# Moving one matmul operand, and all that lies behind it in on-chip memory, to rounder start addresses

## The chip, the cores and the metric

The kernel runs on one core of one Trainium2 chip. Its on-chip memory (SBUF) has 128 partitions, and a tile is a stretch of bytes that begins at the same address in each of them. TensorE (PE) multiplies, VectorE (DVE), ScalarE (ACT) and GpSimd (POOL) work element by element, SyncE (SP) issues the weight transfers. The metric is the device time of one execution in microseconds (us), as the median of three runs.

## The reference, cut to what is computed

Two transformer blocks over 512 tokens of 1024 channels, in float32. The first block runs two layers of feed-forward, a mixer of three attention branches, feed-forward; the second is one layer of a dilated attention mixer with a convolution, and a feed-forward. The feed-forward is the bulk of the work:

```
def swiglu_ffn(x, g, w_gu, w_down):
    h = rms_norm(x, g)
    gate, up = jnp.split(h @ w_gu, 2, axis=-1)
    return (jax.nn.silu(gate) * up) @ w_down
...
for l in range(DEPTH):                                   # first block, DEPTH = 2
    x = x + 0.5 * swiglu_ffn(x, ffn1_norm[l], ffn1_w_gu[l], ffn1_w_down[l])
    x = x + hybrid_mixer(rms_norm(x, mix_norm[l]), ...)  # q, k, v, gates: all products of h
    x = x + 0.5 * swiglu_ffn(x, ffn2_norm[l], ffn2_w_gu[l], ffn2_w_down[l])
...
x = x + rms_norm_2(merged @ w_mix_out, g_post_mix)       # second block, one layer
x = x + rms_norm_2(swiglu_ffn_2(h, w_ffn_in, w_ffn_out), g_post_ffn)
```

## The kernel before

**Tiles.** Three tiles share each partition. `ar` holds matmul operands of type float32r (the ring of prepared weights at R_W, the feed-forward's inner values at R_O, keys and queries). `af` holds float32: weight staging at A_ST, constants at A_C, parameters, small statistics at A_SM, then x at A_X (4096 elements) and scratch behind it at A_Y. In the attention stages the same place behind A_X holds other scratch (M_IQ to M_DQ, and for the second block a list of names U, A, S, P, B, V, PT, T). `h` is the transposed, normalized activation that most products read: eight chunks of 128 channels by 512 tokens, first the high parts, then the low parts. The build puts `ar` at byte 16512 of a partition, `af` at 125056 (both multiples of 128), and `h` at 196384, which is 32 above a multiple of 128. x begins at 147744, 32 above a multiple of 64; of the second block's scratch U does too, and what stands behind U begins 16 above a multiple of 64.

**Products.** `mm3` (L168 to L174) makes one product of a 128x128 weight tile with a chunk of 512 tokens in float32's precision by three matmuls: weight high with activation high (L172), weight high with activation low (L173), weight low with activation high (L174). The weight tile is loaded as the stationary operand, the activation streams as the moving one. In the feed-forward (`gen_ffn`, L244) `up` streams `h`, and `down` streams the inner values from `ar`. Each of five feed-forwards has 22 chunks x 2 x 8 x 3 = 1056 matmuls that stream `h`. Each of the two mixers (`gen_mix`, L386) has 30 units of 24 (`tunit`, L437), the second block's mixer (`gen_mix2`, L1021) 68 units of 24, its output product (`gen_merge2`, L1366) 192. The `group` units of the mixer turn it round: there `h` is the stationary operand and the weights stream.

**Order.** Weights come in 550 units of 512 KB. SP loads a unit into staging, ACT copies it to the ring (L141), DVE makes the low part (L142); the loop is tied to how far the products have come. The order on each engine is fixed when the kernel is built. In the mixers the attention (side stream) is woven into the products (main stream). `bias_rows` (L1005), in the first feed-forward, computes three small tables `t` in scratch at A_Y + 3584 + 2328 and POOL writes each to DRAM 128 times over (`dr_b`, L1019). In `gen_mix2` DVE filters eight chunks with 31 taps each (L1132), a tap starting 4 bytes behind the one before.

Of the kernel before, what the change touches and what calls it, by code (L numbers as in the profile page):

```python
# [26 lines left out]

# [1 line left out]
R_W = 0  # L29
# [18 lines left out]
A_SM = A_RB + 512  # L48
A_X = A_SM + 328
A_Y = A_X + 4096  # L50
# [10 lines left out]
M_DQ = M_PT + 1024  # L61
A_SIZE = M_DQ + 1024

# [30 lines left out]
def const_r():  # L94
    """Stationaries: -1 where row >= column; -1 all over; identity; the strict-past mask."""
    c = np.zeros((128, 512), np.float32)
    p = np.arange(128)
    c[:, 0:128] = np.where(p[:, None] >= p[None, :], -1.0, 0.0)
    c[:, 128:256] = -1.0
    c[:, 256:384] = np.eye(128)  # L100
    c[:, 384:512] = np.where(p[:, None] < p[None, :], 0.0, NEG)
    return c
# [7 lines left out]
class Build:  # L110
# [10 lines left out]

# [1 line left out]
    def r(self, off, n):  # L123
# [4 lines left out]

# [1 line left out]
    def w_dma(self):  # L130
# [29 lines left out]

# [1 line left out]
    def bank(self, ring):  # L162
# [3 lines left out]

# [1 line left out]
    def mm3(self, out, w, a, start, stop, act_stationary=False):  # L168
# [7 lines left out]
    def split(self, hi, lo, src, scale=None):  # L176
        """hi + lo = src * scale, to float32's precision."""
        if scale is None:
            self.nc.scalar.activation(hi, src, AF.Copy)  # L179
            self.nc.vector.tensor_tensor(lo, src, hi, op=ALU.subtract)  # L180
        else:
            self.nc.scalar.activation(hi, src, AF.Copy, scale=scale)
            self.nc.vector.scalar_tensor_tensor(lo, src, scale, hi, op0=ALU.mult, op1=ALU.subtract)  # L183
# [6 lines left out]

# [1 line left out]
    def sq_acc(self, m, src, acc, tmps, apart=False):  # L192
# [19 lines left out]
    def stats_a(self, accs, ps, eps=1e-6, ts=range(4)):  # L212
        """Column sums of the accs into token-major rstd [128, 4]."""
        nc = self.nc
# [12 lines left out]
    def bcast(self, cols, dg, ps, out):  # L227
        """out[:, t*128 + i] = cols[i, t] on every partition."""
        nc = self.nc
        for t in range(cols.shape[-1]):  # L230
            nc.vector.tensor_scalar_mul(dg[:, 128 * t:128 * t + 128], self.f(A_C + C_ID, 128), cols[:, t:t + 1])
        nc.tensor.matmul(ps, lhsT=self.f(A_C + C_ONE, 128), rhs=dg, start=True, stop=True)
        nc.scalar.activation(out, ps, AF.Copy)
# [8 lines left out]

# [1 line left out]
    def gen_ffn(self, wgu, wdn, l, done, halves=None):  # L244
# [41 lines left out]
        def down(grp, cs):  # L286
# [15 lines left out]
            if grp == 0 or not halves:  # L302
                return
            # the last channels a half of the tokens at a time
            tl = {}
# [21 lines left out]
    def ffn_add(self, gain, last=None):  # L327
        """x += 0.5 * rstd * product; the second half also readies the next operand."""
        nc = self.nc
# [12 lines left out]
    def drive(self, main, side=None):  # L342
        """Program order is priority: the side stream goes first, the main one as far as it is waited for."""
        alive = True
# [17 lines left out]
    def behind(self, first, ins):  # L362
        """A product issues behind the one that opens its bank (the first, when there is none yet)."""
        if first is None:
# [6 lines left out]
    @contextlib.contextmanager  # L371
    def late(self, by):
        """Work that other work goes before where both are ready."""
        tc = self.tc
        p = tc.cur_priority
        tc.cur_priority = max(0, p + by)
        yield
        tc.cur_priority = p
# [5 lines left out]

# [1 line left out]
    def gen_mix(self, l):  # L386
# [68 lines left out]

        # compressed branch: the rows (parity, channel) of its first product's operand
        stk = self.r(R_O + 2048, 6144)
# [60 lines left out]
        for m in range(8):  # L518
            for br in range(3):
# [5 lines left out]
                n += 1  # L525
        # the first branch's part of the merge, in the operand's place
        self.mt = self.h_tile(F32)
# [13 lines left out]
    def merged(self, m):  # L541
        """Where the merge of a chunk of channels gathers."""
        return self.mt[:, 512 * m:512 * m + 512]

    def h_tile(self, dtype=F32R):
        """The products' operand; while none is there, the merge's sums."""
        return self.hp.tile([128, 8192 if dtype == F32R else 4096], dtype, name="h", tag="h")

# [1 line left out]
    def rope(self, x, co, si, h, tmp):  # L550
        """x: [128, b, n, >= 2h], co/si: [128, b, 2h]."""
        nc = self.nc
# [11 lines left out]
    def norm_heads(self, x, nh, gain, sq, sm):  # L564
        """x: [128, nh, 64] in place: rms norm over the last axis, times gain."""
        nc = self.nc
# [14 lines left out]
    def one_gain(g):  # L581
        """The same gain for every head."""
        return lambda x: [(x, g[:, None, :].to_broadcast([g.shape[0], x.shape[1], 64]))]
# [4 lines left out]
    def tpose_dup(self, ps, src, tmp, rep=2):  # L588
        """src [128 tokens, n, d]: each [tokens, d] transposed into a column block, rep times down the partitions."""
        _, n, d = src.shape  # L590
# [7 lines left out]
    def gen_idx(self, l):  # L598
# [61 lines left out]

        # the key of the sparse branch
        dk = g1[:, :, 32:96]
# [5 lines left out]
        self.split(self.r(R_KD, 512), self.r(R_KD + 512, 512), ps)  # L668
        # gates of the three branches
        ng = g1[:, :, 8:32]  # L670
# [43 lines left out]
    def sb_pair(self, hp):  # L714
        """Two heads of the stick-breaking branch, key blocks from the last to the first."""
        nc = self.nc
# [43 lines left out]
    def attn_pair(self, q, k, mask, n, gate, v, out, first):  # L760
        """Two heads over n keys: out[channel, token] += gated softmax times values, a head in each half of the rows."""
        nc = self.nc
# [42 lines left out]
    def q2_prep(self, b, src, nh):  # L805
        """Transposed [hi; lo] queries of one block of tokens: [128, nh * 128]."""
        nc = self.nc
# [27 lines left out]
    def q_prep(self, o, nh, g, sm):  # L835
        """Queries of 4 * nh heads at o: norm and rotation in place."""
        self.norm_heads(self.f(o, 256 * nh).rearrange("p (n d) -> p n d", d=64), 4 * nh,
# [4 lines left out]
    def gen_nsa(self, l):  # L842
# [8 lines left out]
        def prep(b):  # L851
            """Queries, and the compressed branch's numerators, transposed."""
            q2 = self.q2_prep(b, q4[:, b], 8)
# [102 lines left out]

# [1 line left out]
    def gen_merge(self, l, gain):  # L958
# [44 lines left out]

# [1 line left out]
    def bias_rows(self):  # L1005
        """Relative-position bias rows of every head, to DRAM."""
        nc = self.nc
# [107 lines left out]
    def conv(self, c, u):  # L1115
        """Causal depthwise filter of one chunk of channels, a tap at a time in the background."""
        nc = self.nc
# [25 lines left out]
    def gen_attn2(self):  # L1143
# [30 lines left out]
        def tok(g):  # L1174
            """The statistics in DRAM, [token, group, kind, head], as group g's layout has the tokens."""
            d = self.dr_s
# [4 lines left out]
        for hp in range(4):  # L1181
# [23 lines left out]
            if hp < 3:  # L1205
                load_bias(hp + 1)
            # statistics of the three groups meet token by token
            d = self.dr_s
# [93 lines left out]
    def gen_ln(self):  # L1302
        """Layer norm over channels of the filtered signal, silu, split for the product."""
        nc = self.nc
# [33 lines left out]
    def post(self, y, next_gain, rb, ts=range(4), pool=()):  # L1338
        """x += rms_norm(y) * gain, y transposed with the gain already in it, its squares summed."""
        nc = self.nc  # L1340
# [82 lines left out]

# [1 line left out]
    def run(self, upto=99, start=0):  # L1425
        tc, nc, ap = self.tc, self.nc, self.ap
        with tc.tile_pool(name="sb", bufs=1) as sb, tc.tile_pool(name="hp", bufs=1) as self.hp, \
# [56 lines left out]
            o = M  # L1484
            for n, sz in (("U", 1084), ("A", 1024), ("S", 512), ("P", 3840), ("B", 1024), ("V", 1536), ("PT", 1024), ("T", 2048)):
                self.m2[n] = o
# [17 lines left out]
def tile_t(v):  # L1504
    """[..., 1024] -> [128, 8] per vector, side by side."""
    v = np.asarray(v, np.float32).reshape(-1, 8, 128)
# [3 lines left out]
def par_array(inp):  # L1510
    """Small parameters, one [128, PAR] array per phase."""
    out = np.zeros((3, 128, PAR - 80), np.float32)
# [24 lines left out]
def bias_consts():  # L1537
    """Rows of one-hot buckets by position, 383 or 255 long, and what is added: 0, or NEG where no key is."""
    c = np.zeros((32, 2, 3, 384), np.float32)
# [45 lines left out]
```

## Time and profile before

| | |
|---|---|
| median of 3 runs | 3584.28 us (3582.41 to 3585.07) |
| span of the profiled execution | 3581.1 us |
| PE busy | 3481.8 us, 97% |
| DVE, ACT, POOL busy | 2001.0, 1316.6, 320.8 us |
| share of PE on the chain that ended last | 90% |
| of it, the three lines of `mm3` | 81% |

The span runs from the first to the last instruction of the program; the 3.2 us between it and the median lie around it. A matmul's own time in the trace is longer than its share of the engine, since the next one starts while it drains: the pace of PE is read from the starts of neighbours. Operands stand as out<-in, so `pb<-h,ar` is a matmul that reads `h` and `ar`.

### The profile page before, as it was taken

Reading aid. Unit: us, or ns where it says so; the run is one execution under the profiler, and the core shown is the slowest. Engines: PE = TensorE matmul, PEld = TensorE weight load, DVE = VectorE, ACT = ScalarE, POOL = GpSimd, SP = SyncE. Lnnn points to the kernel's source line nnn. Section 1 sums busy time; section 2 is a strip of 40 time slices with the busy share of each in tenths; the row PEclk is TensorE's granted clock in tenths of the full one; section 3 lists DMA queues with packets and bytes.
Section 4 is the critical chain, followed back from the end, with each engine's and each line's share of the span. In section 5 each row is a group of like instructions: output and inputs, shape, how many; then the busy total and the mean of one; then the engine's idle time right before and its main releaser. Section 6 shows DMA issues by size and latency. Waiting matters only on the chain.

```text
span 3581.1 us, 43236 instructions
## 1 busy us (share of the span) xinstructions
PE 3481.8 (97%) x16884; PEld 2802.7 (78%) x16884; DVE 2001.0 (56%) x3733; ACT 1316.6 (37%) x2234; POOL 320.8 (9%) x355
## 2 busy tenths in 40 slices
PE   7899999999999999999999999999999999999997
PEld 5688888776788888888787768888877777878886
DVE  4243488566543344434876666433488988544334
ACT  3222354356332233223544464222334443443222
POOL 2000100011300010001000104000111112210002
PEclk9899999999999999999999999999999999999999
DMA  6722332331322222223322314222332224522221
GB/s 148 116 94 94 119 94 86 103 114 62 121 90 98 94 97 89 99 94 112 95 89 101 114 38 147 94 94 94 114 100 86 81 78 142 182 77 94 95 94 54
DMA packets 100814, 357.05 MB, mean 100 GB/s; under 512 B 14168, under 2 KB 16984, under 8 KB 99808
## 3 DMA queue, kind: packets, MB, share of 16 engines
q1 hardware_dynamic: 81504, 290.49, 24.1%
q0 software_dynamic: 18144, 61.76, 6.8%
q8 instruction: 132, 2.16, 0.2%
q10 hardware_dynamic: 960, 2.04, 0.2%
q14 instruction: 74, 0.61, 0.1%
HBM read 320.05 MB, written 32.08 MB: 98 GB/s over the span
## 4 chain that ended last, share of the span: by engine, by line
PE 90%; issue 3%; DMA 3%; DVE 2%; ACT 1%; POOL 1%; another core or an unknown queue 0%; DVEq 0%; ACTq 0%; POOLq 0%
PE pb L172 27%; PE pb L173 27%; PE pb L174 27%; DMA af<-wst 2%; PE pb L801 1%; PE pb L777 1%; PE pb L793 1%; PE pb L1193 1%; PE pb L737 1%; PE pb L1290 1%; PE pb L1266 1%; PE pb L595 0%; PE pb L756 0%; DMA af<-x 0%; PE pb L751 0%
## 5 line engine op out<-in xcount | busy, mean ns | idle before, releaser
L172 PE MATMUL pb<-h,ar 128*128 128x512 f32 x2848 | 1132.8, 401 | 34.6 <-ACT ar L141 16.4
L141 ACT ACTIVATE ar<-af 128x1024 fp32r<-128x1024 f32 x550 | 582.5, 1059 | 1565.1 <-PE pb L173 993.2
L174 PE MATMUL pb<-h,ar 128*128 128x512 f32 x2848 | 1140.7, 401 | 0.1
L173 PE MATMUL pb<-h,ar 128*128 128x512 f32 x2848 | 1140.1, 400 | 0.0
L142 DVE TENSOR_TENSOR ar<-af,ar 128x1024 fp32r<-128x1024 f32 x550 | 687.2, 1250 | 448.6 <-ACT ar L141 435.6
L172 PEld LDWEIGHTS pb<-h,ar 128*128 128x128 f32 x2848 | 540.8, 190 | 167.3 <-ACT ar L141 17.3
L174 PEld LDWEIGHTS pb<-h,ar 128*128 128x128 f32 x2848 | 540.6, 190 | 130.4 <-issue 3.2
L173 PEld LDWEIGHTS pb<-h,ar 128*128 128x128 f32 x2848 | 540.7, 190 | 129.0 <-issue 3.2
L173 PE MATMUL pb<-ar 128*128 128x512 f32 (+1 forms) x1254 | 484.0, 386 | 1.2 <-DVE ar L183 1.2
L174 PE MATMUL pb<-ar 128*128 128x512 f32 (+1 forms) x1254 | 483.3, 386 | 0.0
L172 PE MATMUL pb<-ar 128*128 128x512 f32 (+1 forms) x1254 | 482.4, 387 | 0.6 <-DVE af L779 0.5
L200 POOL TENSOR_TENSOR af<-af 128x512 f32<-128x512 f32 (+1 forms) x76 | 109.6, 1442 | 1857.6 <-ACT af L198 1846.5
L172 PEld LDWEIGHTS pb<-ar 128*128 128x128 f32 x1254 | 235.7, 188 | 49.8 <-DVE af L779 1.2
L173 PEld LDWEIGHTS pb<-ar 128*128 128x128 f32 x1254 | 235.8, 188 | 48.9 <-DVE ar L183 2.4
L174 PEld LDWEIGHTS pb<-ar 128*128 128x128 f32 x1254 | 235.7, 188 | 46.8
L263 DVE TENSOR_TENSOR af<-pb,af 128x512 f32<-128x512 f32 x110 | 75.7, 691 | 317.2 <-PE pb L174 316.1
L261 DVE TENSOR_TENSOR af<-pb,af 128x512 f32<-128x512 f32 x110 | 75.5, 691 | 264.4 <-PE pb L174 249.3
L1132 DVE SCALAR_TENSOR_TENSOR af<-af 128x512 f32<-128x512 f32 x240 | 179.5, 748 | 3.6
L172 PE MATMUL pb<-ar,h 128*128 128x256 f32 (+1 forms) x448 | 134.1, 299 | 0.0
L173 PE MATMUL pb<-ar,h 128*128 128x256 f32 (+1 forms) x448 | 133.2, 297 | 0.0
L174 PE MATMUL pb<-ar,h 128*128 128x256 f32 (+1 forms) x448 | 132.4, 296 | 0.0
L180 DVE TENSOR_TENSOR ar<-af,ar 128x512 fp32r<-128x512 f32 (+4 forms) x178 | 114.4, 649 | 16.3 <-ACT ar L179 15.6
(236 smaller groups left out, 3185.5 us busy)
## 6 DMA issues: line engine op xcount, KB each, us to landing
af<-wst SPq DMA_DIRECT2D x550, 512.0 KB, 3.3
dr_g<-af POOLq DMA_DIRECT2D x64, 256.0 KB, 2.3
af<-dr_g POOLq DMA_DIRECT2D x24, 512.0 KB, 4.5
dr_x<-af POOLq DMA_DIRECT2D x3, 2048.0 KB, 7.3
af<-dr_x POOLq DMA_DIRECT2D x3, 2048.0 KB, 8.7
dr_b<-af POOLq DMA_DIRECT2D x3, 1536.0 KB, 66.4
h<-dr_g POOLq DMA_DIRECT2D x16, 256.0 KB, 6.0
af<-x POOLq DMA_DIRECT2D x8, 256.0 KB, 12.4
```

What stands on the lines that cost most here:

```text
L141: self.nc.scalar.activation(self.r(o, UNIT), st, AF.Copy)
L142: self.nc.vector.tensor_tensor(self.r(o + UNIT, UNIT), st, self.r(o, UNIT), op=ALU.subtract)
L172: mm(out, lhsT=w[0], rhs=a[0], start=start, stop=False, skip_group_check=True)
L173: mm(out, lhsT=w[0], rhs=a[1], start=False, stop=False, skip_group_check=True)
L174: mm(out, lhsT=w[1], rhs=a[0], start=False, stop=stop, skip_group_check=True)
L180: self.nc.vector.tensor_tensor(lo, src, hi, op=ALU.subtract)
L200: nc.gpsimd.tensor_tensor(acc, acc, t, op=ALU.add)
L261: nc.vector.tensor_tensor(gs[i], pg, rb, op=ALU.mult)
L263: nc.vector.tensor_tensor(gs[i], pu, gs[i], op=ALU.mult)
L737: mm(z[u], lhsT=qk(2 + hp, lk)[rs[u], ks], rhs=qk(hp, lq)[rs[u], 128 * j:512], start=i == 0, stop=False, skip_group_check=True)
L777: opens = self.behind(opens, mm(ps, lhsT=q[u], rhs=k[u][l][:, 0:n], start=opens is None, stop=l == 1, skip_group_check=True))
L1132: nc.vector.scalar_tensor_tensor(a, u[:, j:j + 512], w[:, j:j + 1], a, op0=ALU.mult, op1=ALU.add)
```

## The change

A_X moves up by 8 elements, so x and all scratch behind it begin 32 bytes later; `af` grows by 16 elements at its end besides, so that `h` behind it begins 96 bytes later, at 196480, which is 1535 x 128. x begins at 147776, a multiple of 64. U grows by 4 elements, so that A and what follows begin at multiples of 64 too. What lies in front of A_X, and `ar`, stay where they are. The tables `t` of `bias_rows` go from 187776 (a multiple of 128) to 187808 (32 above one). No instruction is added or removed, and the order on each engine is as before. The diff also drops comments, which are left out here.

```
-A_X = A_SM + 328
+A_X = A_SM + 336
...
-A_SIZE = M_DQ + 1024
+A_SIZE = M_DQ + 1024 + 16
...
-            for n, sz in (("U", 1084), ("A", 1024), ("S", 512), ("P", 3840), ("B", 1024), ("V", 1536), ("PT", 1024), ("T", 2048)):
+            for n, sz in (("U", 1088), ("A", 1024), ("S", 512), ("P", 3840), ("B", 1024), ("V", 1536), ("PT", 1024), ("T", 2048)):
```

## Rows read from the trace of the kernel before

**Rows 1.** The page: busy time, PE and its granted clock in slices, the chain.

```profile
PE 3481.8 (97%) x16884; PEld 2802.7 (78%) x16884; DVE 2001.0 (56%) x3733; ACT 1316.6 (37%) x2234; POOL 320.8 (9%) x355
PEclk9899999999999999999999999999999999999999
PE 90%; issue 3%; DMA 3%; DVE 2%; ACT 1%; POOL 1%; another core or an unknown queue 0%; DVEq 0%; ACTq 0%; POOLq 0%
```

**Rows 2.** Groups by line and shape, PE: operands, count | busy us, mean ns | idle.

```profile
L173 PE MATMUL pb<-h,ar 128*128 128x512 f32 x2848 | 1140.1, 400 | 0.0
L172 PE MATMUL pb<-h,ar 128*128 128x512 f32 x2848 | 1132.8, 401 | 34.6 <-ACT ar L141 16.4 <-ACT h L239 12.7 <-DVE af L470 2.0
L173 PE MATMUL pb<-ar 128*128 128x512 f32 x1210 | 471.5, 390 | 1.2 <-DVE ar L183 1.2
L172 PE MATMUL pb<-ar 128*128 128x512 f32 x1210 | 469.9, 391 | 0.6 <-DVE af L779 0.5
L172 PE MATMUL pb<-ar,h 128*128 128x256 f32 x384 | 110.4, 288 | 0.0
L174 PE MATMUL pb<-ar 128*128 128x256 f32 x44 | 12.6, 287 | 0.0
```

**Rows 3.** Timeline of PE, `up` of a feed-forward: 57 rows (start, duration, line, operands).

```profile
1019.77 0.40 PE L172 MATMUL pb<-h,ar 128*128 128x512 f32 x1
1020.01 0.40 PE L173 MATMUL pb<-h,ar 128*128 128x512 f32 x1
...
1032.89 0.40 PE L174 MATMUL pb<-h,ar 128*128 128x512 f32 x1
```

**Rows 4.** The same in `down` of that feed-forward: 59 rows.

```profile
1269.78 0.39 PE L172 MATMUL pb<-ar 128*128 128x512 f32 x1
1270.01 0.39 PE L173 MATMUL pb<-ar 128*128 128x512 f32 x1
...
1282.93 0.39 PE L173 MATMUL pb<-ar 128*128 128x512 f32 x1
```

**Rows 5.** Stretches, instructions that touch `h` alone: us, PE, PEld, DVE, ACT, POOL.

```profile
0.00:137.00 137.00, 92.13 (x360) 71.17 (x360) 9.57 (x8) 5.71 (x8) 0.00 (x0) 0.89 0.77 122
...
2610.00:3030.00 420.00, 354.78 (x1433) 264.95 (x1432) 0.00 (x0) 0.00 (x0) 0.00 (x0) 1.00 0.29 96
...
3185.00:3560.00 375.00, 251.34 (x1056) 201.20 (x1056) 5.98 (x8) 5.23 (x8) 0.00 (x0) 0.99 0.25 82
```

**Rows 6.** Stretches, all instructions: same columns, then PEclk, DMA share, GB/s.

```profile
0.00:137.00 137.00, 95.86 (x376) 72.92 (x376) 43.99 (x58) 34.88 (x46) 18.98 (x22) 0.89 0.77 122
...
420.00:480.00 60.00, 55.52 (x256) 46.45 (x255) 38.53 (x83) 25.94 (x49) 6.74 (x4) 0.91 0.31 114
...
790.00:990.00 200.00, 192.21 (x1092) 147.95 (x1091) 121.78 (x272) 103.69 (x201) 42.09 (x32) 0.99 0.25 88
...
2610.00:3030.00 420.00, 420.00 (x2139) 320.69 (x2138) 363.41 (x755) 167.84 (x372) 59.42 (x91) 1.00 0.29 96
```

**Rows 7.** The first 137 us: a piece of the chain; ACT's timeline; the transfers of `dr_b`.

```profile
79.85 42.88 DMA af<-wst
122.83 1.06 ACT L141 ACTIVATE ar<-af 128x1024 fp32r<-128x1024 f32 x1 [36.65 <-DMA af<-wst]
DMA to landing us min/median/max: 2.6/3.3/66.4
```

**Rows 8.** Groups by line and shape, DVE.

```profile
L180 DVE TENSOR_TENSOR ar<-pb,ar 128x512 fp32r<-128x512 f32 x26 | 17.8, 686 | 15.3 <-ACT ar L179 15.2
L180 DVE TENSOR_TENSOR ar<-af,ar 128x512 fp32r<-128x512 f32 x142 | 96.6, 685 | 7.3 <-ACT ar L179 6.8
L263 DVE TENSOR_TENSOR af<-pb,af 128x512 f32<-128x512 f32 x110 | 75.7, 691 | 317.2 <-PE pb L174 316.1 <-ACT af L262 1.0
```

**Rows 9.** Timeline of DVE late in `gen_mix2`: taps in a row.

```profile
2987.03 3.90 DVE L1132 SCALAR_TENSOR_TENSOR af<-af 128x512 f32<-128x512 f32 x5
...
2994.12 3.11 DVE L1132 SCALAR_TENSOR_TENSOR af<-af 128x512 f32<-128x512 f32 x4
```

## The prediction

> **What bounds the kernel now.** I read the page first. [...] Next come the groups by line and shape. Matmuls of one shape, 128x512, are of two kinds: 3 x 2848 = 8544 stream `h`, and 3 x 1210 stream `ar`. The first last 400 to 401 ns in the mean, the second 390 to 391 [rows 2]. A duration overlaps the next matmul, so it is no price. For the price I took the timeline of two stretches of the same feed-forward in which PE never waits. Where `h` streams, 57 rows start from 1019.77 to 1032.89: 13.12 / 56 = 0.2343 us each [rows 3]. Where `ar` streams, 59 rows start from 1269.78 to 1282.93: 13.15 / 58 = 0.2267 us each [rows 4]. The instruction, the weights and their ring are the same; only the tile of the moving operand differs. A matmul on `h` costs 7.6 ns more, 3.3%.
>
> What sets `h` apart? Its start is 32 bytes above a multiple of 128, while every operand in `ar` begins at a multiple of 128. Its place in memory is another, too, behind `af`. The trace has no 128x512 float32r matmul that streams from an odd start in the low region or an even one in the high, so it can't part the two. I take the start. If memory were read in blocks larger than 32 bytes, a 2048-byte row that begins in the middle of one would touch one block more. At the pace of `ar`, 512 columns in 226.7 ns, 7.6 ns are 17 columns, or 69 bytes of float32: about the size of such a block. A slower region would have no reason to cost just that. The group products speak to the same: with `h` as the stationary operand and `ar` streaming, a 128x256 matmul lasts 288 ns, against 287 with both in `ar` [rows 2]. So the tile costs where it streams at full rate, and the loading of weights from it is hidden.
>
> **The change part by part.**
>
> (1) `h` at a multiple of 128. No instruction moves; the order is the same on each engine. If the start is the reason, the 8544 matmuls go from 0.2343 to 0.2267 us. The `ar` that I compare with begins at 129 x 128, an odd multiple as `h` now does (1535 x 128), so nothing rounder than 128 is needed for that pace. All of it is 8544 x 0.0076 = 64.9 us; what of it reaches the end goes by stage.
>
> Start: in the first 137 us 360 matmuls stream `h` [rows 5], but PE is busy only 95.86 of 137 us [rows 6]. There the chain runs through a weight transfer that takes 42.88 us to land, and ACT waits 36.65 us for it; the transfers to `dr_b`, up to 66.4 us to land, are under way at the same time [rows 7]. A faster PE waits longer there, so I count nothing for these 360.
>
> Feed-forwards: 5 x 1056 - 360 = 4920 matmuls; the last one shows its 1056 in one stretch [rows 5]. PE is their only limit, and everything else in them hangs on PE's results: 4920 x 0.0076 = 37.4 us, all of it on the path.
>
> The two mixers of the first block: 2 x 30 x 24 = 1440, 10.9 us. Two kinds of stretch there have PE idle, 55.52 of 60 us busy where the mixer begins and 192.21 of 200 where it ends [rows 6], and in between the products are the cover for the attention's steps on DVE and ACT. A cover that is 3% shorter gives some of the gain back as a wait for DVE. From below the gain is half, from above all; I take three quarters, since most of the products lie in stretches in which PE doesn't wait: 8.2 us.
>
> The second block's mixer: 68 x 24 = 1632, 12.4 us. In 420 us PE is never idle, but DVE is busy 363.41 us, 87% [rows 6]. With the 1433 rows of `h` there [rows 5] some 11 us shorter, DVE stands at 363 / 409 = 89%. It is still behind PE on the average, but its evacuations queue behind the taps. Three quarters again, half to all for the bounds: 9.3 us.
>
> The output product: 192 x 0.0076 = 1.5 us, on the path.
>
> Sum: 37.4 + 8.2 + 9.3 + 1.5 = 56.4 us.
>
> (2) x and scratch at multiples of 64, read and written by DVE, ACT and POOL. DVE's subtraction with a 128x512 output takes 686 ns with both ends at round starts, 685 with a source in `af`, 691 with an output in `af` [rows 8]. The taps start 4 bytes apart, so they go through all starts there are: five take 3.90 us, four 3.11, 0.79 for the one between [rows 9]; no start stands out. So DVE gains at most 5 ns an instruction, beside PE, which is worth nothing; if their cover is gone, as at the very end, some twenty of them make 0.1 us. ACT runs 1316.6 us and POOL 320.8 of the span, each 1% of the chain [rows 1]; I have no pair of rows for a start of theirs. A gain or loss of 3%, the share that PE shows, on 2% of 3581 us gives 2 us either way; I take 0, as for DVE.
>
> (3) The tables `t` of `bias_rows` lose their round start: rows of 1536 bytes that began at a multiple of 128 now begin 32 above one. They are read 128 times over by the transfers that hold up the weights in the first 137 us. From below the cost is 0, if memory is read in pieces of 32 bytes or smaller, or the DRAM side is the limit. From above, if it is read in blocks of 128, 12 blocks become 13, and 66.4 us [rows 7] become 71.9: 5.5 us on the path. I take 0, since the bytes moved are the same, and keep 5.5 for the range.
>
> [...]
>
> Span 3581.1 - 56.4 = 3524.7 us. The median lies 3.2 us above the profiled span, so I forecast 3584.3 - 56.4 = 3527.9, say **3528 us**, 1.6% faster. Its own range: all of the 64.9 us and 2 from ACT and POOL give 3517; half of the two mixer terms (5.5 and 6.2), the 5.5 of the tables against it, 37.4 + 5.5 + 6.2 + 1.5 - 5.5 = 45.1, give 3539.
>
> **The rivals.**
>
> The start isn't the reason. Then `h` is slow because of where it lies, or memory is read in small pieces, and the move changes nothing: 3584 us. For it: the trace can't part place from start, and DVE shows that its reads don't care about a start [rows 8, 9]. Against: the price is that of one block, and the loading of weights from the same place is not slower [rows 2]. [...]
>
> The gain is cut. Either a start at 128 wins only half of the 7.6 ns, 56.4 / 2 = 28.2, which gives 3556; or both mixer stages swallow their gain in waits for DVE, 37.4 + 1.5 = 38.9, which gives 3545. For it: DVE's 87% [rows 6]. Against: PE has no idle time there now.
>
> The tables' transfers decide, and the kernel is slower. Place: the first feed-forward, from the issue of the three transfers to the late weights at 122.83 us [rows 7]. Price: 5.5 us by blocks of 128, 3590 us. It decides only if `h` gains less than those 5.5 us, that is with the rival of no gain; to be slower by more than 0.2% the reads would have to be 11% slower. A slower pace of `h` itself, which would cost more, I leave out: `ar` has the same phase as the new `h` and is the faster.
>
> **How the numbers follow.** Forecast 0.75; cut gain 0.09; no gain 0.12; slower 0.04. The range goes from 3516, the lower end of the forecast with 1 us for the runs' own spread, to 3557, the end of the cut gain: it holds nearly all of 0.84 and leaves out some 0.18. A measurement of this kernel can tell about 0.2%, 7 us, from no change. Faster by over that: 0.75 + 0.09 = 0.84. Within it: 0.12 and half of the last, 0.14. Slower by more: 0.02.
>
> **What would show it.** In the trace of the changed kernel, matmuls on `h` start 0.2267 us apart and last 390 ns, as those on `ar`; those on `ar` stay. If `h` keeps 0.2343, the start was not the reason and all else falls. The first 137 us stay as long (to within 1 us), with the wait of some 36 us for weights a little longer; a landing of `dr_b` above 68 us would show part 3. DVE's groups keep 685 to 691 ns and their taps 0.79 us of pitch. PE in the second block's mixer shows waits for DVE of 2 to 6 us in all, where it has none now; more than that, and the three quarters were too much.

## The result, and the profile after

The changed kernel takes 3525.73 us (median; 3524.61 to 3530.98) where the kernel before, beside it, takes 3583.35: a ratio of 0.9846 (95% interval 0.9834 to 0.9858), 57.6 us less. The forecast was 3528. The page of the changed kernel, span, busy times and chain, answers to [rows 1]:

```profile
span 3523.7 us, 43236 instructions
PE 3423.5 (97%) x16884; PEld 2793.6 (79%) x16884; DVE 1998.7 (57%) x3733; ACT 1316.1 (37%) x2234; POOL 320.0 (9%) x355
PE 91%; DMA 3%; DVE 3%; ACT 1%; issue 1%; POOL 0%; DVEq 0%; ACTq 0%; POOLq 0%
```

PE lost 58.3 us of busy time, DVE, ACT and POOL 2.3 at most, and the span is shorter by 57.4. So PE still bounds the kernel and has become faster. Where: PE's timeline of the changed kernel, 58 neighbouring matmuls in the stretch of [rows 3] (start, duration, line, operands):

```profile
1007.32 0.39 PE L174 MATMUL pb<-h,ar 128*128 128x512 f32 x1
...
1020.24 0.39 PE L174 MATMUL pb<-h,ar 128*128 128x512 f32 x1
```

12.92 / 57 = 0.2267 us each, where it was 0.2343. That is the pace of `ar` to the last digit [rows 4], and `ar` keeps it (13.37 / 59 = 0.2266 us in the stretch of `down`). The gain is the one that was forecast, in the instruction named.

Where in the program it is gained can be read from instructions that are the same in both kernels. The first of the next rows is the matmul on `h` behind the last long wait of the start; eight more are the first ones on `h` of the stages that follow, and the last is near the end of the program. PE's timeline of the kernel before:

```profile
137.37 0.79 PE L172 MATMUL pb<-h,ar 128*128 128x512 f32 x1 [4.83 <-ACT ar L141]
443.68 0.39 PE L172 MATMUL pb<-h,ar 128*128 128x512 f32 x1
951.27 0.40 PE L172 MATMUL pb<-h,ar 128*128 128x512 f32 x1
1320.10 0.40 PE L172 MATMUL pb<-h,ar 128*128 128x512 f32 x1
1709.54 0.39 PE L172 MATMUL pb<-h,ar 128*128 128x512 f32 x1
2219.27 0.40 PE L172 MATMUL pb<-h,ar 128*128 128x512 f32 x1
2588.10 0.40 PE L172 MATMUL pb<-h,ar 128*128 128x512 f32 x1
3128.04 0.40 PE L172 MATMUL pb<-h,ar 128*128 128x512 f32 x1
3185.21 0.79 PE L172 MATMUL pb<-h,ar 128*128 128x512 f32 x1 [3.37 <-ACT h L239]
...
3569.76 1.22 PE L232 MATMUL pb<-af 128*128 128x256 f32 x2 [8.74 <-DVE af L231]
```

The same ten instructions in the changed kernel:

```profile
136.18 0.79 PE L172 MATMUL pb<-h,ar 128*128 128x512 f32 x1 [4.55 <-ACT ar L141]
437.06 0.39 PE L172 MATMUL pb<-h,ar 128*128 128x512 f32 x1
941.14 0.39 PE L172 MATMUL pb<-h,ar 128*128 128x512 f32 x1
1301.98 0.39 PE L172 MATMUL pb<-h,ar 128*128 128x512 f32 x1
1683.19 0.39 PE L172 MATMUL pb<-h,ar 128*128 128x512 f32 x1
2187.96 0.39 PE L172 MATMUL pb<-h,ar 128*128 128x512 f32 x1
2548.81 0.39 PE L172 MATMUL pb<-h,ar 128*128 128x512 f32 x1
3079.27 0.39 PE L172 MATMUL pb<-h,ar 128*128 128x512 f32 x1
3135.70 0.80 PE L172 MATMUL pb<-h,ar 128*128 128x512 f32 x1 [3.37 <-ACT h L239]
...
3512.33 1.22 PE L232 MATMUL pb<-af 128*128 128x256 f32 x2 [8.75 <-DVE af L231]
```

The lead of a row pair less that of the pair before it is the gain of the stage between them:

| stage | matmuls on `h` | gain, us | per matmul, ns | forecast, us |
|---|---|---|---|---|
| up to 137.37 us | 360 | 1.2 | | 0 |
| rest of the first feed-forward, four more | 696 + 4 x 1056 | 5.4 + 8.0 + 8.2 + 8.0 + 7.9 = 37.5 | 7.6 | 37.4 |
| first block's two mixers | 1440 | 3.5 + 5.0 = 8.5 | 5.9 | 8.2 |
| second block's mixer | 1632 | 9.5 | 5.8 | 9.3 |
| output product, and what follows it | 192 | 0.7 | | 1.5 |
| sum | 8544 | 57.4 | | 56.4 |

Three of these gains hold more than the pace of `h`, since TensorE's granted clock and its waits didn't fall on the same instructions in the two executions. In the second of the two mixers, 1.4 us of the 5.0 are the clock's: from 1774.7 to 1778.1 us of the kernel before it was 0.50, and of the fifteen group products there most took some 213 ns to the next start, where the changed kernel has the full clock and 119 ns. In the last feed-forward the clock of the kernel before is still 0.5 up to 3191.3 us; seven matmuls on `h` take about 426 ns there that take 227 after, a gain of 1.3 us. Against it, the faster PE of the changed kernel catches up twice with ACT's making of `h` (the longer wait is 0.34 us, before 3161.45) and loses 1.1 us around these waits. The third is the output product, below.

### The profile page after: what moved, and what is told of

Read it like the earlier page. It is cut to its first block, busy times and chain, and to the rows that moved or that the text cites. A ratio compares the mean times of both kernels' runs of the same rounds, so it can differ in the third digit from the quotient of the medians.

```text
span 3523.7 us, 43236 instructions
## 1 busy us (share of the span) xinstructions
PE 3423.5 (97%) x16884; PEld 2793.6 (79%) x16884; DVE 1998.7 (57%) x3733; ACT 1316.1 (37%) x2234; POOL 320.0 (9%) x355
## 4 chain that ended last, share of the span: by engine, by line
PE 91%; DMA 3%; DVE 3%; ACT 1%; issue 1%; POOL 0%; DVEq 0%; ACTq 0%; POOLq 0%
PE pb L172 27%; PE pb L173 27%; PE pb L174 27%; DMA af<-wst 2%; PE pb L801 2%; PE pb L793 1%; PE pb L777 1%; PE pb L1193 1%; PE pb L595 1%; PE pb L737 1%; PE pb L1290 1%; PE pb L1266 1%; PE pb L756 0%; DVE af L1351 0%; DVE ar L142 0%
## 5 line engine op out<-in xcount | busy, mean ns | idle before, releaser
L172 PE MATMUL pb<-h,ar 128*128 128x512 f32 x2848 | 1114.2, 394 | 33.9 <-ACT ar L141 15.1
L174 PE MATMUL pb<-h,ar 128*128 128x512 f32 x2848 | 1120.1, 393 | 0.1
L173 PE MATMUL pb<-h,ar 128*128 128x512 f32 x2848 | 1119.4, 393 | 0.0
## 6 DMA issues: line engine op xcount, KB each, us to landing
dr_b<-af POOLq DMA_DIRECT2D x3, 1536.0 KB, 63.3
```

Source lines behind the costliest of these rows:

```text
L172: mm(out, lhsT=w[0], rhs=a[0], start=start, stop=False, skip_group_check=True)
L173: mm(out, lhsT=w[0], rhs=a[1], start=False, stop=False, skip_group_check=True)
L174: mm(out, lhsT=w[1], rhs=a[0], start=False, stop=stop, skip_group_check=True)
```

## The experiments

The theory on record was the *start* of `h`: at a multiple of 128 bytes a row streams at 0.2267 us. The first rivals were the place of `h` in memory, and x with its scratch. After the first eight runs a third theory stood against it: what counts is the *distance* from the weights' start to the start of the moving operand. Weight tiles lie at multiples of 512 bytes from the ring's start, rows of `h` at multiples of 2048 from its own, so the distance modulo 256 is the same for all products of one kind. It is written here as (moving start - weights' start) modulo 256. Before the change it is 196384 - 16512 = 702 x 256 + 160, so 160; after it 196480 - 16512 = 703 x 256, so 0; of the inner values in `ar`, which begin at 57472, 160 x 256, so 0.

Edits are shown against the changed kernel if nothing else is said, and add nothing to the program but room. All orders of instructions stay. A measured time stands with its ratio to the kernel before, run beside it, and the 95% interval. A pace is read from the starts of 58 (`h`) or 60 (`ar`) neighbours, in the stretches of [rows 3, 4].

**h_alone: the move of `h` without the rest** (against the kernel before).

```
-A_SIZE = M_DQ + 1024
+A_SIZE = M_DQ + 1024 + 24
```

> The kernel before with h alone moved to a multiple of 128 (196480); x, all scratch and the tables t stay where they were. If the start of h is the reason for the whole gain: 3526 us, as the changed kernel, matmuls on h 0.227 us apart. If x and scratch have a share: between 3526 and 3584, by as much as they have. If it isn't h at all: 3584 us and 0.234 us.

Measured: 3524.41 us, 0.9841 (0.9825 to 0.9857), `h` at 0.2267. All of the gain is in the move of `h`; x, scratch and tables add nothing that can be measured.

**x_alone: the rest without it.** x and scratch stay at their new starts, `h` goes to 196512.

```
-A_SIZE = M_DQ + 1024 + 16
+A_SIZE = M_DQ + 1024 + 24
```

> The changed kernel with h pushed 32 bytes further (196512), so that it starts 32 above a multiple of 128 again; x, U and what follows keep their round starts. If the start of h is the reason: 3584 us, matmuls on h 0.234 us apart, DVE's 128x512 groups 685 to 691 ns. If x and scratch carry a part of the gain: lower than 3580 us. If the place of h were the reason (further from where it was, on the side of the change): 3526 us.

PE's timeline of x_alone, 58 rows:

```profile
1018.97 0.40 PE L174 MATMUL pb<-h,ar 128*128 128x512 f32 x1
...
1032.27 0.39 PE L174 MATMUL pb<-h,ar 128*128 128x512 f32 x1
```

Measured: 3574.16 us, 0.9982 (0.9973 to 0.9991). 128 bytes further up than before, at the same phase by 128, `h` doesn't have the same pace: 13.30 / 57 = 0.2333, 1 ns better than before. That small gain isn't x's, as h_160 shows below.

**h_64: `h` at 196416, a multiple of 64 alone.**

```
-A_SIZE = M_DQ + 1024 + 16
+A_SIZE = M_DQ + 1024
```

> The changed kernel with h at 196416, a multiple of 64 that is not one of 128; x and scratch as in the change. If a moving operand is read in pieces of 64 bytes (the price of 7.6 ns is about 69 bytes at the matmul's pace): 3526 us and 0.227 us. If the pieces are of 128 bytes: 0.234 us and 3584 us, as with 32. If the cost grows with the distance from a multiple of 128: in between, some 3550 us.

PE's timeline of h_64, 58 rows:

```profile
1019.38 0.39 PE L174 MATMUL pb<-h,ar 128*128 128x512 f32 x1
...
1032.68 0.40 PE L174 MATMUL pb<-h,ar 128*128 128x512 f32 x1
```

Measured: 3572.1 us, 0.9973 (0.9964 to 0.9983); 13.30 / 57 = 0.2333. 64 won't do. By blocks of 64 it should have.

**ar_32: the inner values off, the ring and `h` in place.** R_O moves up by 32 bytes to 57504; `h` is put back to 196480.

```
-R_O = R_W + RING * 2 * UNIT
+R_O = R_W + RING * 2 * UNIT + 8
-R_SIZE = R_CON + 512
+R_SIZE = R_CON + 512 + 24
-A_X = A_SM + 336
+A_X = A_SM + 320
-A_SIZE = M_DQ + 1024 + 16
+A_SIZE = M_DQ + 1024
```

> The changed kernel with everything in ar behind the weight ring moved 32 bytes off a multiple of 128 (the inner values that the down products stream, queries, keys); the weight ring and h keep their round starts, x lies at 147840. If the start is the reason, it holds in the low region too: the matmuls that stream ar go from 0.227 to 0.234 us, 3 x 1210 x 0.0075 = 27 us, 3553 us, while those on h stay at 0.227. If it was the place of h: ar stays at 0.227, 3526 us.

PE's timeline of ar_32, `down`, 60 rows:

```profile
1259.25 0.40 PE L174 MATMUL pb<-ar 128*128 128x512 f32 x1
...
1273.02 0.39 PE L173 MATMUL pb<-ar 128*128 128x512 f32 x1
```

Measured: 3553.25 us, 0.9921 (0.9906 to 0.9935). Now `ar` has the slow pace, 13.77 / 59 = 0.2334, and `h` the fast one, 0.2267. The place in memory is out as a cause: a tile in the low region slows down when its start is moved. 3 x 1210 x 6.7 ns = 24 us is about what this kernel loses against the changed one, 27.5.

Up to here the start explains all but the odd 1 ns between 160 and 32, and that 64 doesn't do. Of the runs that follow, w_64, ar_256, all_32 and w_32 part start from distance. (160 and 32 are distances here. In the name and the expectation of h_160, 160 is how far `h` begins above a multiple of 256; its distance is 32.)

**h_160: `h` at 196512 again, x and scratch as before** (against the kernel before).

```
-A_SIZE = M_DQ + 1024
+A_SIZE = M_DQ + 1024 + 32
```

> The kernel before with h alone pushed 128 bytes further (196512: still 32 above a multiple of 128, but 160 above one of 256 in place of 32). It tells what made the matmuls on h 0.2333 us with x and scratch round and h at 196512, against 0.2342 before. If it was the start of h by 256: 0.2333 us here too, 3575 us. If it was x and scratch: 0.2342 us, 3582 us.

Measured: 3571.88 us, 0.9970 (0.9960 to 0.9979), `h` at 13.31 / 57 = 0.2335. x_alone's few us come from the start of `h`, not from x. And the distances 160 and 32, equal by 128, differ: 234.3 ns before against 233.3 and 233.5 in x_alone and h_160.

**w_64: the weights move.** The ring goes up by 64 bytes, to 16576; the inner values by 128, to 57600; `h` stays at 196480.

```
-R_W = 0
-R_O = R_W + RING * 2 * UNIT
+R_W = 16
+R_O = R_W + RING * 2 * UNIT + 16
-A_X = A_SM + 336
+A_X = A_SM + 320
-A_SIZE = M_DQ + 1024 + 16
+A_SIZE = M_DQ + 1024
```

> The changed kernel with the weight ring alone moved 64 bytes off a multiple of 128 (its start in ar at 16576); the inner values, h (196480) and x keep round starts, x lies at 147840. If the loading of weights is hidden under the streams, as the prediction has it: 3526 us, both paces 0.227 us. If the stationary operand's start counts too and costs like the moving one's: up to 12174 x 0.0065 = 79 us more, 3605 us. The groups with h as stationary went from 0.1197 to 0.1169 us when h lay 64 off; if that holds for the weights of 512-column matmuls as well, 12174 x 0.0028 = 34 us less, 3492 us.

PE's timeline of w_64: 58 rows of `h`, 60 of `ar`:

```profile
1016.37 0.40 PE L174 MATMUL pb<-h,ar 128*128 128x512 f32 x1
...
1029.67 0.39 PE L174 MATMUL pb<-h,ar 128*128 128x512 f32 x1
...
1266.31 0.39 PE L174 MATMUL pb<-ar 128*128 128x512 f32 x1
...
1279.81 0.39 PE L173 MATMUL pb<-ar 128*128 128x512 f32 x1
```

Measured: 3578.13 us, 0.9992 (0.9983 to 1.0002). `h` begins where it does in the changed kernel and has lost all but 1 ns of its gain: 13.30 / 57 = 0.2333. `ar` begins at a multiple of 128 too and runs at 13.50 / 59 = 0.2288. The weights' address is half of the matter. The distances are 192 for `h`, the same as in h_64 with the same 0.2333, and 64 for `ar`.

**ar_256: ring and inner values up by 128 bytes**, so all starts are multiples of 128. The distance of `h` is 128, that of `ar` 0.

```
-R_W = 0
+R_W = 32
-A_X = A_SM + 336
+A_X = A_SM + 320
-A_SIZE = M_DQ + 1024 + 16
+A_SIZE = M_DQ + 1024
```

> The changed kernel with all of ar moved by 128 bytes (16640), so that the weight ring, the inner values, queries and keys begin at multiples of 256; h stays at 196480, an odd multiple of 128. If 128 is all that counts, as the prediction has it: both paces 0.227 us, 3526 us. If 256 is better still: matmuls on ar under 0.227 while those on h stay, and some us less.

PE's timeline of ar_256, 58 rows of `h`:

```profile
1013.65 0.40 PE L174 MATMUL pb<-h,ar 128*128 128x512 f32 x1
...
1026.89 0.39 PE L174 MATMUL pb<-h,ar 128*128 128x512 f32 x1
```

Measured: 3567.88 us, 0.9960 (0.9946 to 0.9974). 13.24 / 57 = 0.2323 for `h`, 0.2267 for `ar`. Every start is as the forecast wants it, and three quarters of the gain are gone. So the start by 128 is not the reason; and the distance doesn't repeat after 128.

**t_round: the tables `t` at a multiple of 128 again**, all else as changed.

```
-            t = self.f(o + 2328 + 384 * g, 384)[0:8]
+            t = self.f(o + 2352 + 384 * g, 384)[0:8]
```

> The changed kernel with the tables t of bias_rows moved by 96 bytes to a multiple of 128 again. With t at a round start the first product after the start's wait for weights began at 61.1 and 60.3 us, with t 32 off at 62.4 to 64.0. If the start of t is the reason: 60.7 us (within 0.7), and the end about 2 us earlier, 3523 us. If that was chance or x's doing: 62 to 64 us, 3526 us.

Measured: 3526.86 us, 0.9850 (0.9836 to 0.9865). The longest landing of `dr_b` is 61.0 us, against 63.3 in the changed kernel, and the first product behind the wait for weights starts at 61.99 us, against 62.55. But h_160, with round tables as well, has 65.1 and 63.21, and the kernel before 66.4 us [rows 7] with an earlier start, 61.07. Over all the runs the start lies between 60.25 and 63.21 with round tables and between 61.79 and 64.01 without. An effect of the tables is not shown; if there is one, it is within this spread.

**all_32: everything 32 bytes off, all distances kept.** The ring begins at 16544, the inner values at 57504, `h` at 196512: none at a multiple of 64.

```
-R_W = 0
+R_W = 8
```

> The changed kernel with the weight ring, and with it everything behind it in ar, all of af and h, pushed on by 32 bytes: every operand starts 32 off a multiple of 128, and all distances between them are as in the change. If the start of the moving operand counts, as the prediction had it: 0.233 us on h and on ar, some 12174 x 0.0064 = 78 us more than the change, 3604 us. If the distance between the stationary and the moving operand by 256 bytes counts, which the four runs before suggest (ar_256: 0.2327 us on an h that starts round, 128 from the ring's phase; w_64 and h_64: 0.2333 us both, 192 from it): 0.227 us on both, 3526 us.

PE's timeline of all_32: 58 rows of `h`, 60 of `ar`:

```profile
1004.70 0.39 PE L174 MATMUL pb<-h,ar 128*128 128x512 f32 x1
...
1017.62 0.39 PE L174 MATMUL pb<-h,ar 128*128 128x512 f32 x1
...
1248.82 0.39 PE L174 MATMUL pb<-ar 128*128 128x512 f32 x1
...
1262.20 0.39 PE L173 MATMUL pb<-ar 128*128 128x512 f32 x1
```

Measured: 3523.68 us, 0.9840 (0.9825 to 0.9855). 12.92 / 57 and 13.38 / 59, 0.2267 and 0.2268: the whole gain, with no operand at a round start. `h` lies here at 196512, where it ran at 0.2333 in x_alone and h_160.

**w_32: the counterpart.** The ring begins at 16544, the inner values at 57600, `h` at 196480: both moving operands at multiples of 128, no distance at 0.

```
-R_W = 0
-R_O = R_W + RING * 2 * UNIT
+R_W = 8
+R_O = R_W + RING * 2 * UNIT + 24
-A_X = A_SM + 336
+A_X = A_SM + 320
-A_SIZE = M_DQ + 1024 + 16
+A_SIZE = M_DQ + 1024
```

> The changed kernel with the weight ring at 16544, the inner values at 57600, h at 196480: by 256 bytes the moving operand lies 96 from the weights where it is in ar, and 224 where it is h, the two distances not measured yet. If the start of the moving operand counts: both are at multiples of 128, 0.227 us, 3526 us. If the distance counts: neither is at 0, and as 64 took 0.2290 us and 32, 128, 160 and 192 took 0.2327 to 0.2342, both lie between 0.229 and 0.234 us, 3550 to 3600 us; under 0.227 us on one of them would make a distance that is better than 0.

PE's timeline of w_32, 58 rows of `h`:

```profile
1019.02 0.40 PE L174 MATMUL pb<-h,ar 128*128 128x512 f32 x1
...
1032.32 0.40 PE L174 MATMUL pb<-h,ar 128*128 128x512 f32 x1
```

Measured: 3593.69 us, 1.0039 (1.0026 to 1.0051), slower than before: 13.30 / 57 = 0.2333 for `h`, and 0.2332 for `ar`, whose distance was 0 before. all_32 and w_32 settle it: round starts of the streaming operands are neither needed nor enough. The full pace, 0.2266 to 0.2268 us, was there at distance 0 in every stretch read, whatever the starts, and at none of the other seven multiples of 32.

## Why the prediction was right, and where it was wrong

**The number holds, the reason doesn't.** The median came 2 us below the forecast. The step that failed is "What sets `h` apart? ... I take the start." The runs put in its place the distance between the weights and the row that streams, modulo 256. Before the change it was 160 for `h`, and the change, written to make starts rounder, happened to make it 0.

**The argument by size of a block was a coincidence.** It read 7.6 ns as 69 bytes, one block touched more. By that a row at a multiple of 128 would have cost nothing; in w_64 both kinds of rows begin at one, and `ar` takes 228.8 ns and `h` 233.3. A row that all_32 starts 32 above a multiple of 64 takes 226.7.

**"Nothing rounder than 128 is needed"** was read from the start of `ar`, 129 x 128. What that row had was the distance 0 from the ring, in the same tile. ar_256 is the case that the sentence excluded: an `h` at a multiple of 128, and 232.3 ns.

**"The loading of weights from it is hidden"** misled, though the time of those loads with `h` as the weights hardly differs (190 ns each before, 191 after). The group products have no slow kind beside them for a reason that was not seen: with `h` as the weights they had a distance as well (96), and at 256 columns it costs nothing against 0 (119.8 ns before, 119.7 after, from start to start). The weights' address is half of what sets the pace of the matmul that streams, as w_64 and w_32 show by moving the ring and not `h`.

**The rival "a slower pace of `h`", which was left out**, rested on the same sentence, "`ar` has the same phase as the new `h`". It was right that it has, by 128 and by 256; but w_32 shows a layout whose streaming operands start as round and that is slower than before, there by `ar`, which has lost its distance 0; `h` is 1 ns faster in it than before. The argument didn't hold, and the case was left out on it.

**The terms.** The feed-forwards gave 37.5 us for 37.4 forecast, and in the first four the gain is all on the path, as said. In the last it was not quite: 1.1 us went into waits for `h`, and the clock happened to give 1.3 back. Of the 37.5, 0.5 us isn't from rows of `h` that stream: the 192 group products of 448 columns, which stand between the feed-forwards and the first matmul on `h` of each mixer, went from 205.3 to 202.7 ns, a term that the prediction put at nothing. The 360 matmuls of the start gave 1.2 for 0; the first 137 us differ by more than that from run to run. The output product gave 0.7 for 1.5: its 192 matmuls gained 7.6 ns each, 1.46, but of the sixteen small column sums behind them (L218) the last eight took 0.7 us longer, at a mean granted clock of 0.55 where it was 1.00. PE's timeline, the kernel before, then the changed one:

```profile
3175.30 1.05 PE L218 MATMUL pb<-af 128*128 128x1 f32 x8 [1.33 <-ACT af L198]
3125.08 1.75 PE L218 MATMUL pb<-af 128*128 128x1 f32 x8 [1.34 <-ACT af L198]
```

In all_32, with the same pace of `h`, they have the full clock and take 1.05 us again, so this 0.7 isn't the price of the change.

**The mixers' three quarters were met for another reason.** Named was a cover that gets too short, with 2 to 6 us of PE waiting for DVE in the second block's mixer, "where it has none now". PE's waits in that stage (2560 to 3070 us) of the changed kernel, line, releaser, total, times and longest:

```profile
PE pb L172 <- DVE af L1066: 2.0, 1, 2.0
PE pb L172 <- DVE af L1097: 1.8, 1, 1.8
```

In the kernel before the same two are 2.0 and 1.6 us, at 2608.82 and 3038.43 us, just outside the stretch from 2610 to 3030 in which the prediction saw no wait. So no more than 0.2 us was given back. What is missing stands behind the attention's products. PE's timeline in that mixer, changed kernel, after a run of nine short products:

```profile
2619.09 0.88 PE L1193 MATMUL pb<-ar 64*128 64x128 f32 x9
2619.90 0.50 PE L173 MATMUL pb<-h,ar 128*128 128x512 f32 x1
2620.24 0.39 PE L174 MATMUL pb<-h,ar 128*128 128x512 f32 x1
...
2621.63 0.39 PE L174 MATMUL pb<-h,ar 128*128 128x512 f32 x1
...
2625.25 0.39 PE L172 MATMUL pb<-h,ar 128*128 128x512 f32 x1
```

The first takes 0.34 us to the next start, the next six 1.39 / 6 = 0.2317 each, and only then comes 3.62 / 16 = 0.2263. Of the 1632 matmuls on `h` in this mixer, 1185 reach 226.7 ns after the change and gain 8.9 us together; 295 have their next start 229 to 245 ns later, 232.5 in the mean (233.9 before), and gain 0.4; the 152 at the edges gain 0.2. So the gain is whole where products of `h` follow one another for long, and nearly nil in the first few behind other products. Why the pace takes so long to come back is open.

The first block's mixers show the same. PE is idle there for 13.0 and 13.4 us before and for 13.1 and 12.0 after, so nothing was given back as waits; of the 1440 matmuls on `h`, 804 reach a next start under 229 ns and gain 5.9 us. Where the clock is full in both kernels, all that stream `h` gain 7.0 us. That the stage shows 8.5, so near the forecast of 8.2, is in part the clock's doing and luck.

**Parts 2 and 3.** x and scratch gave 0 as said: DVE's groups of [rows 8] take 687, 685 and 690 ns after, its taps 748 in both, and h_alone has the whole gain. One group on POOL became faster, the eight additions of L1389 (1438 ns, 1582 before), but it has 1439 in h_alone too, with x where it was, so it isn't x's start. The sign named for the tables, a landing of `dr_b` above 68 us, came in no run (67.5 at most), and the wait for weights that was to grow from 36.65 us is 34.58 after; no cost of the tables is shown, and 5.5 us was too wide a bound. In t_round, with round tables, the first product behind the wait starts 0.56 us earlier, which lies within the spread.

## What to carry to other kernels

When matmuls of one shape have two paces, compare where their *two* operands lie, relative to each other, before looking at either alone. Here a streaming operand whose rows begin at the same phase modulo 256 bytes as the weight tiles is 1% to 3% faster at 512 columns than at any other distance tried (226.8 to 227.3 ns against 229.0 to 234.2), also where both begin 32 above a multiple of 128 (all_32). So pad by the distance, and look at it again whenever any tile in front changes size. A change that does what was forecast has not yet shown why: only a layout that keeps the named cause and takes away the other (ar_256), and one that does the reverse (all_32), part two causes that the change moved together.

## What the runs showed of the hardware

The pace of a 128x512 float32r matmul with a weight load for each, by the distance modulo 256, as the mean start to start of all neighbours of a run but those more than 25 ns off the median; distances that are no multiples of 32 were not tried:

| distance | ns | where |
|---|---|---|
| 0 | 226.8 to 227.3 | `ar` before, after, ar_256 and all_32; `h` after, h_alone, t_round, ar_32, all_32 |
| 32 | 233.3 | `h` in x_alone and h_160, `ar` in ar_32 |
| 64 | 229.0 | `ar` in w_64 |
| 96 | 233.4 | `ar` in w_32 |
| 128 | 232.7 | `h` in ar_256 |
| 160 | 234.2 | `h` before |
| 192 | 233.3 | `h` in h_64 and in w_64 |
| 224 | 233.3 | `h` in w_32 |

Whole multiples of 256 made no difference here: `h` after the change lies 703 x 256 from the ring and the inner values 160 x 256, and both have the full pace, 0.2267 and 0.2266 us. At 256 columns the order is another. In the mixer's group products `h` is the stationary operand and the ring streams; their distance is 0 in the changed kernel and 64 in h_64. PE's timeline of the changed kernel, 83 of them:

```profile
1774.72 0.33 PE L172 MATMUL pb<-ar,h 128*128 128x256 f32 x1
...
1784.59 0.28 PE L173 MATMUL pb<-ar,h 128*128 128x256 f32 x1
```

The same 83 in h_64:

```profile
1800.83 0.33 PE L172 MATMUL pb<-ar,h 128*128 128x256 f32 x1
...
1810.18 0.28 PE L173 MATMUL pb<-ar,h 128*128 128x256 f32 x1
```

9.87 / 82 = 0.1204 us against 9.35 / 82 = 0.1140: in this stretch the distance 0 is the slower one, by 5%. Over all such neighbours of the two runs it is 119.7 against 116.9 ns, 2.4%. No start of `h` tried serves both: h_64 is the layout that is better for these, and with the 8544 long ones at 233.3 ns it takes 3572.1 us.

Why the pace hangs on the distance is not shown: no run took the loads of weights away, and a kernel in which several matmuls share one load wasn't tried. What is shown is that the address of the weights reaches the pace of the matmul that streams: 226.7 ns for `h` after the change and 233.3 in w_64, with the same loads and `h` at the same start. Whether it is the loads that do it, no run shows.
